# Five features of the mix stored as rounded and low parts, and two output tiles that take turns

## The chip, the cores and the metric

The kernel runs on one core of a Trainium2 chip. The metric is the time of one execution on the device in microseconds (us). Of the kernel before, three runs and one profiled execution are at hand. Its engines are TensorE (PE, with its weight loads as PEld), VectorE (DVE), ScalarE (ACT), GpSimd (POOL) and SyncE (SP); each works through its own instructions in order, and they meet at semaphores. Transfers between DRAM and the on-chip memory are DMAs, issued here from SP and POOL.

## The reference

Two encoder layers over 1040 frames of width 1024. In each layer a normed input goes through one projection whose columns serve two groups of heads: four gated-linear-attention heads (features 0 to 3 of the mix, 128 wide each) and eight softmax heads with a forget bias (FoX), which give features 4 to 7. The mix is what goes through the output projection `w_out`:

```python
xn = rms_norm(h, attn_norm[i])
gq, gk, gv, gr, glr, fq, fk, fv, ff = jnp.split(xn @ w_in[i], cuts, axis=-1)
o_gla = rms_norm(gla_chunk_causal(...), gla_norm[i]...) * jax.nn.silu(gr)
o_fox = rms_norm(forgetting_attention(...), fox_norm[i]...)
h = h + jnp.concatenate([o_gla, o_fox], axis=-1) @ w_out[i]
h = h + conv_ffn(rms_norm(h, ffn_norm[i]), w_up[i], conv_w[i], conv_b[i], w_down[i])
```

All of it is in float32.

## The kernel before

A float32 product is made of three matmuls of a rounded type (`mm3`, L241 to L243): each operand is split into a part `hi`, rounded by a cast on ACT, and a part `lo`, the rest, subtracted on DVE; PE then adds hi x hi, hi x lo and lo x hi. `split` (L366, L367, and with a scale L369, L370) does it for activations, `weights` (L208, L210) for weights. Features lie on the partitions (128 of them), frames along the rows.

The attention of a layer runs in `fox` as a fixed series of steps: four pairs of FoX heads, eighteen steps a pair, in five groups of query tiles (the last group has one tile). A step issues scores (`S`, L686, L687), DVE adds the bias row `cb` and keeps the running minimum (`P` and `m`, L694), ACT takes the exponential, PE transposes (`tr`, L723), ACT and DVE split the transposed block (`PT`), and PE multiplies with the values (`av`, L741). At the end of a group `fox_fold` transposes and norms (`fo`, `ff`), and two steps later `fox_store` transposes once more and writes the feature of the pair. The masks of `cb` run on POOL. PSUM tiles `S`, `tr` and `fo` share a ring of five buffers, the tile `mm` has two.

Between these steps stands filler work, so that PE does not run dry: `plan(p)` gives a list of units when pair p begins. A unit (`unit`) is one output tile of 128 columns over one chunk of frames and is taken matmul by matmul between the attention's own instructions. With pairs 0 to 2 the filler makes the projections of the next pair and the gate of head p (`gr_products`, with the gate's own chain `gx`, `ge`, `gy`, `gog` on DVE and ACT, L646 to L657); with pair 3, the gate of head 3. When that is done `plan(4)` gives the first four output tiles of `w_out` (`NSPLIT`), each over chunks of 256, 384 and 400 frames, and over seven of the eight features in the order KORD = (4, 5, 0, 1, 2, 3, 6). Feature 7, that of pair 3, is added later, in the next stage.

The mix gets there through DRAM: `fox_store` (L787, L788) and the gate (L657, L659) write each feature as float32 to `mixd[k]`; with `plan(3)` five of them are loaded into `land` on POOL (L970), feature 6 comes in chunks in `plan(4)` (L975), and feature 3 never leaves the chip. In `plan(4)` all seven are split, chunk by chunk, 21 splits (`mh` on ACT L366, `ml` on DVE L367) in each layer. The first output tile carries them: two splits are issued ahead of a unit (FEED = 2), then one with each feature. The residual stream is loaded into the same `land` tiles behind the split (L991, POOL) and added when the output is read from PSUM (L996). The next tile's weights are asked for when the first unit of a tile starts.

The instructions of each engine are recorded in the order in which this code issues them, but for the scores, which are moved up by some places.

## Time and profile before

| | us |
|---|---|
| median of three runs | 2553.93 |
| the runs | 2550.85, 2553.93, 2555.95 |
| profiled execution | 2549.59 |
| its span | 2547.7 |
| mean granted clock of PE | 0.994 |
| PE, DVE, ACT, POOL busy | 2483.9, 1748.1, 1273.1, 405.1 |

Times in the trace run from the start of the span. The attention of layer 0 ends near 500, that of layer 1 near 1790. Pair 3 of layer 0 begins near 412, and its `plan(4)` near 455. A row of the timeline reads: start, duration, engine, line, operation, what it writes and reads, and in brackets how long the engine stood idle before it and what ended that.

### The profile page before, as it was taken

The page shows a single profiled execution, that of the slowest core. Times are in us where ns is not written, and L with a number is a line of the kernel's source. Part 1 is how long each engine was busy: PE and PEld are TensorE (multiplying, and loading weights), DVE is VectorE, ACT ScalarE, POOL GpSimd, SP SyncE. Part 2 cuts the span into 40 slices and gives each one's busy share as a digit, 9 for nine tenths or more (in the row PEclk, how much of TensorE's full clock was granted, in tenths as well). Part 3 has the DMA queues.
Part 4 walks back from the last instruction along what each step waited for, and adds up shares of the span by engine and source line. Part 5 has one row for each costly group of instructions (what it writes and reads, how often), then busy time and mean ns, then how long its engine had stood idle before and what let it go on. Part 6 is the DMA issues. An engine that isn't in the chain of part 4 may idle for free.

```text
span 2547.7 us, 48524 instructions
## 1 busy us (share of the span) xinstructions
PE 2483.9 (97%) x19278; PEld 2420.5 (95%) x19278; DVE 1748.1 (69%) x3389; ACT 1273.1 (50%) x2582; POOL 405.1 (16%) x580
## 2 busy tenths in 40 slices
PE   8999999999999999999999999999999999999998
PEld 7989999998999999999999899999999999999997
DVE  7655676769877777853565666777697777777535
ACT  7346666646544445641343466665464444455412
POOL 4033333210000000100210333331100000001002
PEclk9999999999999999999999999999999999999999
DMA  3232134342322224764312222142523222258622
GB/s 122 71 86 73 39 95 129 114 152 78 107 86 78 81 80 127 201 161 116 106 50 72 74 79 68 66 148 95 169 74 110 75 76 87 76 158 187 187 70 76
DMA packets 118515, 260.91 MB, mean 102 GB/s; under 512 B 14880, under 2 KB 32544, under 8 KB 118288
## 3 DMA queue, kind: packets, MB, share of 16 engines
q1 hardware_dynamic: 95136, 184.36, 23.2%
q0 software_dynamic: 22432, 72.71, 10.4%
q8 instruction: 151, 2.47, 0.4%
q10 hardware_dynamic: 720, 0.74, 0.1%
q14 instruction: 76, 0.62, 0.1%
HBM read 177.16 MB, written 67.81 MB: 96 GB/s over the span
## 4 chain that ended last, share of the span: by engine, by line
PE 65%; issue 17%; DVE 11%; DMA 3%; ACT 3%; POOL 1%; SPq 0%; DVEq 0%; POOLq 0%; ACTq 0%
PE mm L241 8%; PE mm L243 7%; PE mm L242 7%; PE up L242 5%; PE up L241 5%; PE up L243 5%; PE down L241 5%; PE down L242 5%; PE down L243 5%; PE av L741 3%; PE tr L723 2%; DVE P L694 2%; DVE x L1085 1%; PE wo L241 1%; PE S L686 1%
## 5 line engine op out<-in xcount | busy, mean ns | idle before, releaser
L241 PE MATMUL up<-x,hi 128*128 128x260 f32 (+1 forms) x2464 | 699.2, 284 | 8.0 <-ACT hi L1060 4.9
L243 PE MATMUL up<-x,hi 128*128 128x260 f32 (+1 forms) x2464 | 698.0, 283 | 2.1 <-DVE x L1085 2.1
L242 PE MATMUL up<-x,lo 128*128 128x260 f32 (+1 forms) x2464 | 698.5, 283 | 1.3 <-DVE lo L1061 1.3
L241 PEld LDWEIGHTS up<-x,hi 128*128 128x128 f32 x2464 | 466.6, 189 | 9.7 <-ACT hi L1060 5.3
L243 PEld LDWEIGHTS up<-x,hi 128*128 128x128 f32 x2464 | 467.0, 190 | 3.0 <-DVE x L1085 2.9
L242 PEld LDWEIGHTS up<-x,lo 128*128 128x128 f32 x2464 | 466.5, 189 | 2.0 <-DVE lo L1061 1.8
L1061 DVE TENSOR_TENSOR lo<-raw,hi 128x512 fp32r<-128x512 f32 x364 | 247.6, 685 | 173.4 <-ACT hi L1060 173.4
L241 PE MATMUL mm<-xh,hi 128*128 128x348 f32 (+4 forms) x1056 | 363.4, 344 | 0.0
L243 PE MATMUL mm<-xl,hi 128*128 128x348 f32 (+4 forms) x1056 | 340.0, 322 | 0.0
L242 PE MATMUL mm<-xh,lo 128*128 128x348 f32 (+4 forms) x1056 | 339.5, 321 | 0.0
L1060 ACT CAST hi<-raw 128x512 fp32r<-128x512 f32 x364 | 224.3, 620 | 145.5 <-PE up L243 84.9
L241 PEld LDWEIGHTS mm<-xh,hi 128*128 128x128 f32 x1056 | 200.0, 189 | 6.3 <-issue 5.3
L242 PEld LDWEIGHTS mm<-xh,lo 128*128 128x128 f32 x1056 | 200.0, 189 | 0.6 <-issue 0.3
L243 PEld LDWEIGHTS mm<-xl,hi 128*128 128x128 f32 x1056 | 198.8, 188 | 0.9 <-issue 0.7
L208 ACT CAST hi<-raw 128x512 fp32r<-128x512 f32 (+2 forms) x184 | 106.6, 582 | 185.0 <-PE down L243 113.0
L242 PE MATMUL down<-ah,lo 128*128 128x260 f32 (+1 forms) x704 | 198.0, 281 | 0.6 <-DVE lo L210 0.5
L243 PE MATMUL down<-al,hi 128*128 128x260 f32 (+1 forms) x704 | 198.1, 281 | 0.0
L241 PE MATMUL down<-ah,hi 128*128 128x260 f32 (+1 forms) x704 | 198.0, 281 | 0.0
L367 DVE TENSOR_TENSOR PT<-tr,PT 116x464 fp32r<-116x464 f32 (+3 forms) x240 | 122.3, 515 | 71.3 <-ACT PT L366 69.2
L702 ACT ACTIVATE P<-P,m 116x924 f32<-116x924 f32 (+4 forms) x144 | 110.5, 767 | 75.0 <-DVE m L694 69.4
L723 PE MATMUL tr<-ident,P 116*116 116x116 f32 x704 | 144.0, 268 | 2.3 <-DVE m L694 1.8
L1268 POOL DMA_DIRECT2D actd<-cv x44 | 23.6, 536 | 766.5 <-DVE cv L1267 745.5
(283 smaller groups left out, 5768.3 us busy)
## 6 DMA issues: line engine op xcount, KB each, us to landing
raw<-in_wm_dram SPq DMA_DIRECT2D x330, 256.0 KB, 2.9
raw<-in_wd_dram SPq DMA_DIRECT2D x64, 256.0 KB, 3.7
actd<-cv POOLq DMA_DIRECT2D x22, 520.0 KB, 3.0
actd<-cv POOLq DMA_DIRECT2D x22, 512.0 KB, 3.1
cb<-cd SPq DMA_DIRECT2D x16, 520.0 KB, 4.2
st<-actd SPq DMA_DIRECT2D x14, 520.0 KB, 5.1
st<-actd SPq DMA_DIRECT2D x14, 512.0 KB, 5.9
kA<-kA SPq DMA_DIRECT2D x24, 260.0 KB, 4.4
```

The source lines that it names most:

```text
L208: nc.scalar.copy(hi[:, :n, :], raw[:, :n, :])
L241: nc.tensor.matmul(ps, wh, xh[:, c0:c0 + n], start=first, stop=False, skip_group_check=more)
L242: nc.tensor.matmul(ps, wl, xh[:, c0:c0 + n], start=False, stop=False, skip_group_check=more)
L243: nc.tensor.matmul(ps, wh, xl[:, c0:c0 + n], start=False, stop=last, skip_group_check=more)
L367: nc.vector.tensor_tensor(out=lo, in0=src, in1=hi.bitcast(F32), op=ALU.subtract)
L686: nc.tensor.matmul(S[:rows, :n], q["qA"][e][:, qs], q["kA"][e][:, c0:k1], start=True, stop=False)
L694: nc.vector.tensor_tensor_reduce(out=x, in0=S[:rows, :n], in1=cb[:rows, c0:k1], scale=1.0, scalar=(BIG if ci == 0 else m[:rows, ci - 1:ci] ...
L702: nc.scalar.activation(x, x, AF.Exp, scale=-1.0, bias=low, accum_out=(den if nch < 3 else d2[:rows, 0:1]))
L723: nc.tensor.transpose(tr[:w, j, :rows], P[:rows, o:o + w], id_)
L741: nc.tensor.matmul(av[:, a:width], w.rearrange("p a b -> p (a b)"), x, start=(t == 0 and i == 0), stop=(t == last and i == 1))
L1060: nc.scalar.copy(hi[:, :nk, :], src[:, :nk, :])
L1061: nc.vector.tensor_tensor(out=lo[:, :nk, :], in0=src[:, :nk, :], in1=hi[:, :nk, :].bitcast(F32), op=ALU.subtract)
```

## The change

Five features, PARTS = (4, 5, 0, 2, 6), are split where they are produced. In `fox_store` of pairs 0 to 2 ACT writes the rounded part to `fst` as before and DVE the low part into `on`, which is the tile `ff` of the fold (one buffer); in the gates of heads 0 and 2 ACT casts into `gog` and DVE subtracts into `gy` (one buffer). Two DMAs write the parts to `mixh` and `mixl`. With `plan(3)` six full loads bring the parts of 4, 5 and 0 straight into `mh` and `ml`, with one load for feature 1; in `plan(4)` twelve loads from SP bring features 2 and 6 chunk by chunk. Features 1 and 3 are still split in `plan(4)`: 6 splits instead of 21.

The first two output tiles take turns chunk by chunk. FEED = 8 issues the splits of a chunk in one go, and the second tile's units carry those of the chunk after. The next tile's weights are asked for in the last chunk of the second tile (`wait`, `left`).

```diff
@@ -53,3 +53,4 @@
 NSPLIT = 4
-FEED = 2
+PARTS = (4, 5, 0, 2, 6)
+FEED = 8
 N_DMA_SUM = 5
@@ -176,3 +177,4 @@
         self.hd = [dp.tile([128, T], F32, name=f"hd{k}") for k in range(KD)]
-        self.mixd = [dp.tile([128, T], F32, name=f"mixd{k}") for k in range(KD)]
+        self.mixd = dp.tile([128, T], F32, name="mixd1")
+        self.mixs = {k: [dp.tile([128, T], F32, name=f"mix{x}{k}") for x in "hl"] for k in PARTS}
         self.ogd = [dp.tile([128, T], F32, name=f"ogd{k}") for k in range(4)]
@@ -256,4 +258,4 @@
             f()
-        if not box.get("ahead"):
-            box["ahead"] = True
+        box["left"] = box.get("left", box["wait"] + 1) - 1
+        if box["left"] == 0:
             nxt = box["work"].after(box)
@@ -273,9 +275,17 @@
 
-    def add_tile(self, work, pp, src, xs, chunks, evac, ks=range(KD), w=None, feed=None, vec=False):
-        box = {"src": src, "work": work, "vec": vec}
-        if w is not None:
-            box["w"] = w
-        work.boxes.append(box)
+    def add_tile(self, work, pp, src, xs, chunks, evac, ks=range(KD), w=None, vec=False):
+        self.add_tiles(work, pp, [(src, evac, w, {})], xs, chunks, ks, vec)
+
+    def add_tiles(self, work, pp, tiles, xs, chunks, ks, vec):
+
+        boxes = []
+        for src, evac, w, feed in tiles:
+            box = {"src": src, "work": work, "vec": vec, "wait": len(chunks) - 1 if boxes else 0}
+            if w is not None:
+                box["w"] = w
+            boxes.append(box)
+        work.boxes += boxes
         for j, (c0, n) in enumerate(chunks):
-            work.add(self.unit(pp, box, src, ks, xs, c0, n, evac, (feed or {}).get(j, ())), len(ks) * 3 * mm_us(n))
+            for box, (src, evac, w, feed) in zip(boxes, tiles):
+                work.add(self.unit(pp, box, src, ks, xs, c0, n, evac, feed.get(j, ())), len(ks) * 3 * mm_us(n))
 
@@ -657,4 +667,9 @@
             nc.vector.scalar_tensor_tensor(out=to, in0=y, scalar=-1.0, in1=og, op0=ALU.mult, op1=ALU.mult)
-            if dst is None:
-                nc.gpsimd.dma_start(self.mixd[h][:, c0:c0 + n], e)
+            if h in PARTS:
+                parts = og, y
+                self.split(*(x.bitcast(F32R) for x in parts), e)
+                for d, x in zip(self.mixs[h], parts):
+                    nc.gpsimd.dma_start(d[:, c0:c0 + n], x)
+            elif dst is None:
+                nc.gpsimd.dma_start(self.mixd[:, c0:c0 + n], e)
         self.add_tile(work, pp, self.wm[lyr, M_GR + h], nm["x"], CH_FOX if dst is None else CH_FOX[::-1], ev)
@@ -785,5 +800,7 @@
             return
-        st = ap.tile([128, 2 * FT], F32, tag="fst", name="fst", bufs=1)
-        nc.scalar.mul(st[:, :n], trf[:, :n], self.v(lyr, V_XN, p))
-        nc.gpsimd.dma_start(self.mixd[4 + p][:, c0:c0 + n], st[:, :n])
+        parts = [x[:, :n] for x in (ap.tile([128, 2 * FT], F32, tag="fst", name="fst", bufs=1),
+                                    on.rearrange("p a b c -> p (a b c)"))]
+        self.split(*(x.bitcast(F32R) for x in parts), trf[:, :n], self.v(lyr, V_XN, p))
+        for d, x in zip(self.mixs[4 + p], parts):
+            nc.gpsimd.dma_start(d[:, c0:c0 + n], x)
 
@@ -957,2 +974,5 @@
                 box = {}
+
+                def part_slots(k):
+                    return s.get(F32R, f"mh{k}"), s.get(F32R, f"ml{k}")
                 KORD = (4, 5, 0, 1, 2, 3, 6)
@@ -967,10 +987,11 @@
                     elif p == 3:
-                        land = box["land"] = [s.get(F32, f"h{k}") for k in range(KD - 1)]
-                        for k in (4, 5, 0, 1, 2):
-                            nc.gpsimd.dma_start(land[k][:, :T], self.mixd[k][:])
+                        mix = box["mix"] = {k: part_slots(k) for k in PARTS[:3]}
+                        land = box["land"] = {k: s.get(F32, f"h{k}") for k in (3, 1)}
+                        for k in PARTS[:3]:
+                            for x, d in zip(mix[k], self.mixs[k]):
+                                nc.gpsimd.dma_start(x[:, :T].bitcast(F32), d[:])
+                        nc.gpsimd.dma_start(land[1][:, :T], self.mixd[:])
                         self.gr_products(lyr, 3, w, ap, pp, nm, land[3])
                     elif p == 4:
-                        land = box["land"]
-                        for c0, n in reversed(CH):
-                            nc.gpsimd.dma_start(land[6][:, c0:c0 + n], self.mixd[6][:, c0:c0 + n])
+                        mix, hT = box["mix"], box["land"]
                         for x in nm["x"]:
@@ -978,4 +999,18 @@
                         s.put(nm["r"])
-                        mix = box["mix"] = [(s.get(F32R, f"mh{k}"), s.get(F32R, f"ml{k}")) for k in range(KD)]
-                        hT = box["hT"] = land + [s.get(F32, "h7")]
+                        for k in (2, 6):
+                            mix[k] = part_slots(k)
+                        for c0, n in CH[::-1]:
+                            for k in (2, 6):
+                                for x, d in zip(mix[k], self.mixs[k]):
+                                    nc.sync.dma_start(x[:, c0:c0 + n].bitcast(F32), d[:, c0:c0 + n])
+                        mix[1] = part_slots(1)
+                        hT[0] = s.get(F32, "h0")
+                        mix[3] = part_slots(3)
+                        hT[2] = s.get(F32, "h2")
+                        mix[7] = part_slots(7)
+                        for k in range(4, KD):
+                            hT[k] = s.get(F32, f"h{k}")
+                        mix = box["mix"] = [mix[k] for k in range(KD)]
+                        hT = box["hT"] = [hT[k] for k in range(KD)]
+                        land = hT
                         ready = self.weights(self.wm[lyr, M_WO], vec=True)
@@ -991,9 +1026,12 @@
                                     nc.gpsimd.dma_start(hT[m][:, c0:c0 + n], hsrc[m][:, c0:c0 + n])
-                            return [lambda k=k: one(k) for k in KORD] + [residual]
-                        for m in range(NSPLIT):
-                            def ev(ps, c0, n, m=m):
+                            return [lambda k=k: one(k) for k in KORD if k not in PARTS] + [residual]
+                        def out_tile(m):
+                            def ev(ps, c0, n):
                                 h = hT[m][:, c0:c0 + n]
                                 nc.vector.tensor_tensor(out=h, in0=ps, in1=h, op=ALU.add)
-                            first = {} if m else {"w": ready, "feed": {j: split(2 - j) for j in range(3)}}
-                            self.add_tile(w, pp, self.wm[lyr, M_WO + m], mix, chunks[::-1], ev, ks=KORD, vec=True, **first)
+                            feed = {0: split(2)} if m == 0 else {j: split(1 - j) for j in range(2)} if m == 1 else {}
+                            return self.wm[lyr, M_WO + m], ev, None if m else ready, feed
+                        self.add_tiles(w, pp, [out_tile(0), out_tile(1)], mix, chunks[::-1], KORD, True)
+                        for m in range(2, NSPLIT):
+                            self.add_tiles(w, pp, [out_tile(m)], mix, chunks[::-1], KORD, True)
                     return w
```

How the order moves is shown at three places, all of layer 0.

The first is the start of the output projection on PE. `mm_6178` is the first tile over 256 frames; the rows begin with the last matmul of its last feature, 6, and run on into the next unit. Before:

```order
L243 MATMUL mm_6178<-ml6_6114,hi_6126 128x256
L723 MATMUL tr_6228<-ident_61,P_6030 116x116
L686 MATMUL S_6236<-kA0_4630,qA0_4628 116x460
L687 MATMUL S_6236<-kL0_4632,qA0_4628 116x460
L723 MATMUL tr_6228<-ident_61,P_6030 116x116 x3
L241 MATMUL mm_6247<-mh4_6109,hi_6126 128x384
```

The changed kernel (`mm_6244` is the first tile, `mm_6303` the second, both over 256 frames):

```order
L245 MATMUL mm_6244<-ml6_6155,hi_6188 128x256
L738 MATMUL tr_6280<-ident_61,P_6084 116x116
L701 MATMUL S_6288<-kA0_4660,qA0_4658 116x460
L702 MATMUL S_6288<-kL0_4662,qA0_4658 116x460
L738 MATMUL tr_6280<-ident_61,P_6084 116x116 x3
L243 MATMUL mm_6303<-mh4_5826,hi_6240 128x256
```

Around the scores nothing moves; behind them stands the second tile's chunk of 256 frames with the same `mh` and `ml` in place of the first tile's chunk of 384.

On DVE at the same place, up to the read of the scores that fill the buffer which the scores above take (`P_6154` before). `ml` rows are splits; `fa`, `fy`, `ff` belong to the fold. Before:

```order
L367 TENSOR_TENSOR ml2_6106<-h2_5779,mh2_6105 128x256
L312 TENSOR_TENSOR fa_6059<-fa_6059,fv_6056 116x4
L367 TENSOR_TENSOR ml3_6108<-h3_5780,mh3_6107 128x256
L313 SCALAR_TENSOR_TENSOR fy_6058<-fa_6059,fy_6058 116x4
L654 SCALAR_TENSOR_TENSOR ge_6086<-ge_6086,gy_6089 128x344
L769 TENSOR_TENSOR ff_6052<-ff_6052,fy_6058 116x128 x2
L655 SCALAR_TENSOR_TENSOR gy_6089<-ge_6086,gy_6089 128x344
L694 ISA P_6154,m_6150<-S_6151,cb_5485 116x460
```

The changed kernel (the read is `P_6216`):

```order
L377 TENSOR_TENSOR ml1_6169<-h1_5833,mh1_6168 128x384
L323 SCALAR_TENSOR_TENSOR fy_6112<-fa_6113,fy_6112 116x4
L377 TENSOR_TENSOR ml3_6172<-h3_5832,mh3_6171 128x384
L784 TENSOR_TENSOR ff_6106<-ff_6106,fy_6112 116x128 x2
L664 SCALAR_TENSOR_TENSOR ge_6140<-ge_6140,gy_6143 128x344
L709 ISA P_6216,m_6212<-S_6213,cb_5523 116x460
```

In front of the read stand four splits now, of features 1 and 3 for two chunks; before, it was seven. Behind the read and four rows more of the gate and the same scores the changed kernel has

```order
L377 TENSOR_TENSOR PT0_6202<-tr_6204,PT0_6202 116x4x116
L377 TENSOR_TENSOR ml1_6169<-h1_5833,mh1_6168 128x400
L377 TENSOR_TENSOR ml3_6172<-h3_5832,mh3_6171 128x400
L777 SCALAR_TENSOR_TENSOR fd_6437<-den_5861 116x4
L377 TENSOR_TENSOR PT1_6203<-tr_6264,PT1_6203 116x3x116
L1031 TENSOR_TENSOR h0_6170<-mm_6244,h0_6170 128x256
L709 ISA P_6291,m_6287<-S_6288,cb_5523 116x460
L709 ISA m_6287 116x1
L377 TENSOR_TENSOR PT0_6202<-tr_6280,PT0_6202 116x4x116
```

with the 400-frame splits of features 1 and 3 ahead of the `PT0` that the next `av` waits for; before, five splits stood there, and nine more behind it.

The second place is the end of pair 0 on DVE (`ff_3431` and `ff_3448` are the folds of its last group, `ge` and `gy` the gate's chain), with what each row waits for. Before:

```order
L657 SCALAR_TENSOR_TENSOR ge_3370<-gy_3373,gog_3368 128x348 [waits DVE_49]
L758 TENSOR_TENSOR ff_3431<-fo_3428,ff_3431 112x128 [waits Activation_49]
L646 TENSOR_TENSOR gx_3467<-mm_3383,r_149 128x348 [waits PE_49]
L367 TENSOR_TENSOR PT1_3323<-tr_3448,PT1_3323 116x4x116 [waits Activation_49]
L764 TENSOR_REDUCE fv_3435<-fo_3428 112x2 [waits Activation_49]
L653 TENSOR_TENSOR gog_3464<-gx_3467,gog_3464 128x348 [waits DMAHW7_49,DVE_49]
L765 TENSOR_TENSOR fv_3435<-fv_3435,fd_3436 112x2 [waits DVE_49]
L762 SCALAR_TENSOR_TENSOR fd_3746<-den_3193 116x4 [waits DVE_49]
L311 SCALAR_TENSOR_TENSOR fa_3438<-fy_3437 112x2 [waits Activation_49]
L649 TENSOR_SCALAR ge_3466<-gx_3467 128x348 [waits DMASW7_49]
```

The changed kernel:

```order
L667 SCALAR_TENSOR_TENSOR ge_3382<-gy_3385,gog_3380 128x348 [waits DVE_49]
L380 SCALAR_TENSOR_TENSOR ff_3312<-tr_3437,vec_59,fst_3440 128x232 [waits Activation_49]
L377 TENSOR_TENSOR PT1_3335<-tr_3465,PT1_3335 116x4x116 [waits Activation_49]
L377 TENSOR_TENSOR gy_3385<-ge_3382,gog_3380 128x348 [waits Activation_49]
L656 TENSOR_TENSOR gx_3484<-mm_3398,r_152 128x348 [waits PE_49]
L659 TENSOR_SCALAR ge_3483<-gx_3484 128x348 [waits DVE_49]
L663 TENSOR_TENSOR gog_3481<-gx_3484,gog_3481 128x348 [waits DMAHW7_49,DMASW0_49]
L773 TENSOR_TENSOR ff_3448<-fo_3445,ff_3448 112x128 [waits DMASW3_49,Activation_49]
L709 ISA P_3533,m_3529<-S_3530,cb_3196 116x460 [waits PE_49]
```

Two rows come in, the low parts of the fox store (`ff_3312`) and of the gate (`gy_3385`); the add of the fold moves down by six rows, and it now waits for a DMA too (DMASW3, the store of `ff_3312`). The `ge` of the next chunk no longer waits for a store.

The third place is the start of pair 3 on POOL, from the first load of a feature. Before:

```order
L970 DMA h4_5781<-mixd4_94 128x1040 [waits DMASW4_49,PE_49]
L970 DMA h0_5777<-mixd0_90 128x1040 [waits DMASW5_49]
L210 TENSOR_TENSOR lo_5825<-raw_5822,hi_5824 128x512 [waits DMAHW1_49,Activation_49]
L970 DMA h5_5782<-mixd5_95 128x1040 [waits DMASW6_49,DMAHW2_49,DMASW1_49,PE_49]
L859 TENSOR_TENSOR cb_5485<-cb_5485,mask_66 116x116 [waits DMAHW1_49,DVE_49,Pool_49]
L970 DMA h1_5778<-mixd1_91 128x1040 [waits DMASW7_49,DMASW0_49]
```

The changed kernel:

```order
L992 DMA mh5_5828<-mixh5_93 128x1040 [waits DMASW5_49,DMASW3_49,PE_49]
L992 DMA mh4_5826<-mixh4_91 128x1040 [waits DMASW4_49,PE_49]
L992 DMA mh0_5830<-mixh0_95 128x1040
L876 TENSOR_TENSOR cb_5523<-cb_5523,mask_66 116x116 [waits DMAHW1_49,DVE_49,Pool_49]
L992 DMA ml4_5827<-mixl4_92 128x1040 [waits DMASW6_49,PE_49]
L992 DMA ml5_5829<-mixl5_94 128x1040 [waits DMASW7_49]
```

Three loads stand ahead of the first mask of `cb` in both; in the changed kernel the low part of a weight tile no longer stands between them, and two more full loads follow behind the mask.

## The prediction

> **What bounds the kernel now.** The page comes first, then the windows of 10 us, then the chain of waits and the timeline of the places where a window shows TensorE idle.

> ```profile
> PE 2483.9 (97%) x19278; PEld 2420.5 (95%) x19278; DVE 1748.1 (69%) x3389; ACT 1273.1 (50%) x2582; POOL 405.1 (16%) x580
> ```

> TensorE (PE) is busy for 97% of the span, and the change takes no matmul away: 17561 rows of PE stand in the order before and after. All that can be won is idle time of PE, 63.8 us in a span of 2547.7, and time lost to a lowered clock. So I looked for the windows in which PE is idle near the code that the change touches (columns: busy us and count of PE, PEld, DVE, ACT, POOL, then the granted clock, the DMA share and GB/s).

> ```profile
> 460.00:470.00 10.00, 6.38 (x50) 5.64 (x48) 9.96 (x32) 10.00 (x28) 2.23 (x5) 1.00 0.53 166
> 470.00:480.00 10.00, 10.00 (x60) 9.70 (x61) 9.93 (x26) 4.18 (x13) 4.66 (x9) 0.83 0.50 155
> 1720.00:1730.00 10.00, 6.37 (x48) 5.79 (x48) 9.97 (x32) 10.00 (x29) 1.71 (x3) 0.85 0.48 150
> ```

> In each layer there is one window (460 to 470, 1720 to 1730) in which PE stands for 3.6 us while DVE and ACT are full: this is the start of the output projection, where the mix features are split. The waits of that stage and the rows of PE around them:

> ```profile
> PE mm L243 <- DVE ml L367: 3.6, 2, 3.0
> ...
> 462.45 0.36 PE L241 MATMUL mm<-mh,hi 128*128 128x256 f32 x1
> 463.95 0.78 PE L741 MATMUL av<-PT,V 116*128 116x232 f32 x6
> 465.94 0.39 PE L243 MATMUL mm<-ml,hi 128*128 128x256 f32 x1 [0.65 <-DVE ml L367]
> 469.94 0.38 PE L243 MATMUL mm<-ml,hi 128*128 128x256 f32 x1 [2.97 <-DVE ml L367]
> 471.73 0.52 PE L243 MATMUL mm<-ml,hi 128*128 128x384 f32 x1
> 472.05 0.52 PE L241 MATMUL mm<-mh,hi 128*128 128x384 f32 x1
> 474.55 0.34 PE L241 MATMUL mm<-mh,hi 128*128 128x384 f32 x1
> 474.73 0.34 PE L242 MATMUL mm<-mh,lo 128*128 128x384 f32 x1
> 1725.05 0.38 PE L243 MATMUL mm<-ml,hi 128*128 128x256 f32 x1 [0.67 <-DVE ml L367]
> 1729.04 0.58 PE L243 MATMUL mm<-ml,hi 128*128 128x256 f32 x1 [2.96 <-DVE ml L367]
> ```

> PE waits for the low part of a split twice, 0.65 and 2.97 us; layer 1 repeats it to 0.02 us. Behind it the clock is down: the 384-column matmuls start 0.32 us apart (471.73, 472.05) until about 474.1, and 0.18 us apart (474.55, 474.73) later. The granted clock of 470 to 480 is 0.83, so 0.17 of 10 us, **1.7 us** more, is lost in a layer. The place costs 3.62 + 1.7 = 5.3 us per layer, 10.6 us in both.

> **The change part by part, the splits first.**

> ```profile
> L367 DVE TENSOR_TENSOR ml<-h,mh x42: 408/545/568, 457.5 to 1737.6; 128x256 fp32r<-128x256 f32 x14, 128x384 fp32r<-128x384 f32 x14, 128x400 fp32r<-128x400 f32 x14
> L366 ACT CAST mh<-h x42: 388/508/544, 428.6 to 1729.8; 128x256 fp32r<-128x256 f32 x14, 128x384 fp32r<-128x384 f32 x14, 128x400 fp32r<-128x400 f32 x14
> L370 DVE SCALAR_TENSOR_TENSOR ml<-tr,vec,mh x10: 332/457/459, 474.5 to 1780.0; 128x232 fp32r<-128x232 f32 x8, 128x112 fp32r<-128x112 f32 x2
> ```

> Of 42 splits at 0.545 us on DVE and 0.508 us on ACT, 30 leave this stage (15 a layer, 8.2 us of DVE, 7.6 us of ACT); 12 stay. They come back as 30 operations of the L370 kind (0.457 us) in the fox pairs and 12 subtractions of about 0.5 us in the gates of heads 0 and 2, where DVE is less full. The count of DVE's work hardly changes; its place does.

> What is late next? In the changed order PE runs the same rows up to the end of the first unit (all seven features need only two splits now), and then meets a scores matmul that waits for DVE's read P of the scores before it. The rows of DVE in that stage:

> ```profile
> 461.72 0.42 DVE L758 TENSOR_TENSOR ff<-fo,ff 116x256 f32<-116x256 f32 x1
> 464.19 1.29 DVE L210 TENSOR_TENSOR lo<-raw,hi 128x512 fp32r<-128x512 f32 x2
> 467.68 0.63 DVE L694 CUSTOM_DVE_ANT_0 P<-S,cb 116x460 f32<-116x460 f32 x1
> 469.48 2.28 DVE L367 TENSOR_TENSOR ml<-h,mh 128x256 fp32r<-128x256 f32 x5
> ```

> Before, P starts at 467.68 with about 3.0 us of splits queued ahead of it since 457; after, four splits of 1.9 us stand there. So P starts about 1.1 us earlier, at 466.6, and is read out near 467.2. PE did four features from 462.45 to 463.95, 0.375 us each, and stood at the fifth at 464.81, after the av group and transposes; three features more and one transpose end at about 466.1. First new wait: **1.1 us**. Second: the next av group on PE waits for a PT split on DVE that stands behind the two 400-column splits, two more PT splits, the residual add and the next P. From 467.2 these sum to about 4.8 us (five at 0.43 to 0.55, two at 0.50, two at 0.3 to 0.35), to 472.0; PE gets there at 470.9. Second new wait: **1.1 us**. Together 2.2 us instead of 3.62: 1.4 us per layer won, with ends of 0 (DVE as late as before) and 3.6 (both waits gone).

> The clock: single stalls near 1.1 us, as these two would be, left it alone.

> ```profile
> 362.12 0.47 PE L686 MATMUL S<-kA,qA 128*116 128x460 f32 x1 [1.03 <-DVE m L694]
> 363.79 0.32 PE L242 MATMUL mm<-xh,lo 128*128 128x344 f32 x1
> 427.88 0.32 PE L741 MATMUL av<-PT,V 112*128 112x112 f32 x1 [1.11 <-DVE PT L367]
> ```

> After 1.03 us of idling the 344-column matmul still takes 0.32 us, as elsewhere at full clock. With 3.7 us of work between the two new waits I count the clock as kept: another 1.7 us a layer, ends 0 and 1.7. The splits' term is therefore 2 x (1.4 + 1.7) = **-6.2 us**.

> [...]

> The loads: features 2 and 6 arrive as parts by 12 loads from SP into slots that PE's last reads of xh0 to xl1 free at about 456.0, and are wanted at 464.8.

> ```profile
> 455.70 0.32 PE L243 MATMUL mm<-xl,hi 128*128 128x344 f32 x1
> 464.81 0.36 PE L241 MATMUL mm<-mh,hi 128*128 128x256 f32 x1
> h<-mixd POOLq DMA_DIRECT2D x1, 128.0 KB, 2.4
> ```

> Four loads of 128 KB, issued by 458 and 2.4 us long, are there by 460.5: hidden by 4 us, **0**. If that cover went, each us beyond 464.8 would stand on PE.

> **Pair ends.** The fold of the fifth group writes the one ff buffer, which now holds the low part of the fourth group's store until its DMA lands; ACT's copy waits for that, DVE's add waits for ACT, and on DVE P stands behind, and PE's next scores behind P. Pairs 0, 1 and 2 of two layers: six places.

> ```profile
> 269.95 0.28 DVE L758 TENSOR_TENSOR ff<-fo,ff 112x128 f32<-112x128 f32 x1
> 270.33 0.55 POOL L659 DMA_DIRECT2D mixd<-ge  x1 [0.61 <-DVE ff L758]
> 275.34 0.34 DVE L649 TENSOR_SCALAR ge<-gx 128x348 f32<-128x348 f32 x1 [2.01 <-DMA mixd<-ge]
> 276.19 0.63 DVE L694 CUSTOM_DVE_ANT_0 P<-S,cb 116x460 f32<-116x460 f32 x1
> 355.48 0.28 DVE L758 TENSOR_TENSOR ff<-fo,ff 112x128 f32<-112x128 f32 x1
> 359.85 0.63 DVE L694 CUSTOM_DVE_ANT_0 P<-S,cb 116x460 f32<-116x460 f32 x1
> DMA to landing us min/median/max: 1.8/3.3/5.3
> ```

> The last row is that of the fox stores (fst). At pair 1 the new operation takes the place of the add at 355.48, so the low part is ready near 355.9, lands 3.3 us later at 359.3, copy and add take 0.6: P at about 360.1, against 359.85, **+0.25 us**. At pair 0 of layer 0 DVE already waited for a store that took 5.0 us (270.33 to 275.34), and the new wait falls on the same time: about 0. I take 4 x 0.25 = **+1.0 us** for the six, with ends of -1.5 (pair 0's wait gone) and 6 x 2.2 = +13 (each store as slow as the slowest, 5.3 us).

> [...]

> **Start of pair 3.** POOL issues three loads of 520 KB ahead of the first mask of cb, as before, but the third without a weight subtraction in front of it, and seven loads in all instead of five.

> ```profile
> cb<-cd SPq DMA_DIRECT2D x16, 520.0 KB, 4.2
> 412.19 1.08 POOL L970 DMA_DIRECT2D h<-mixd  x2 [3.41 <-PE tr L723]
> 413.98 0.33 SPq L830 DMA_DIRECT2D cb<-cd  x1
> 416.27 0.57 POOL L970 DMA_DIRECT2D h<-mixd  x1
> 420.69 0.64 DVE L694 CUSTOM_DVE_ANT_0 P<-S,cb 116x460 f32<-116x460 f32 x1 [0.93 <-DMA cb<-cd]
> ```

> cb took 6.7 us from its issue to P beside these loads, against a median of 4.2 us, and DVE waited 0.93 us for it; PE's stall of 1.11 us at 427.88 lies behind. Three loads cost it 2.5 us, 0.8 us each; the third comes at about 413.3 now, ahead of cb and not 2.3 us behind it, and can cost at most those 0.8 us again, or nothing, if cb has its share of the engines whatever stands in POOL's queue. I take 0.3 us in each layer: **+0.6 us**. Last, the third tile's weights are made only when the second tile is in its last chunk, one unit (about 5 us) before use: two casts and two subtractions of 0.65 us each (L210 above) nearly always fit: **+0.6 us**, ends 0 and 4.

> The sum is -6.2 + 1.0 + 0.6 + 0.6 = **-4.0 us**. The profiled execution took 2549.59 us (span 2547.7 and 1.9 around it), 4.3 us below the median 2553.93 of three runs; I put the difference on the median: **2549.9 us**. About 0.2%, 5.1 us, is what a measurement of this kernel can tell from no change.

> **The rivals.**

> **Both waits vanish.** DVE turns out to be earlier than I add up, since the chain of casts on ACT gets shorter too (ACT is full from 460 to 470). For it: 1.1 us each is small. Then -10.6 + 2.2 = -8.4, 2545.5 us. Chance 0.20.

> **The clock drops all the same**, because the two waits lie 3.7 us apart. For it: between 465.94 and 469.94 two waits were 1 us apart and the clock fell. Against it: the two rows above. -2.8 + 2.2 = -0.6, 2553.3 us. Chance 0.12.

> **The change doesn't do what it says:** the wait for splits comes back whole, as a wait for P or for late part loads, with the clock loss. Then 0 + 2.2: 2556.1 us. Chance 0.10.

> **Slower: the stores hold ff.** At the pair ends the DMA writes of the low parts take as long as the one of 5.0 us at 270.33, two stores instead of one being queued. Each place costs 0.25 us plus what the landing takes over 3.3 us, so 2 us each, about 12 us in all, and -6.2 + 12 + 1.2 = +7.0: 2560.9 us. It is slower by more than 5.1 us from 10.1 us on the six places, 1.7 us each, a landing of 4.75 us. For it: max 5.3 and the stall at 275.34. Against it: the median 3.3. Chance 0.13.

> **How the numbers follow.** My forecast has 0.45; its own range is 2547 to 2553, of which somewhat under two fifths lies below 2548.8 (faster by 0.2%). Faster: 0.17 of it and the 0.20 of the first rival, 0.37. Slower: 0.12 of the last rival and 0.05 of the third, 0.17. The rest, 0.46, is within 0.2%. The range runs from 2544 (first rival with somewhat less given back) to 2559 (third rival), and leaves out most of the last.

> **What would show it.** In the profile after: no wait of mm for ml in the first unit of w_out, one or two waits of about 1.1 us of S for DVE m and of av for PT near 466 and 471, and a granted clock of 1.00 in 470 to 480; ACT's ff copy at 359 waiting for a store of a low part, by how much; P at the start of pair 3 waiting 1.2 us for cb. It is wrong if these waits are over 2 us at the pair ends, or if the windows at 460 and 1720 are as empty as before.

## The result and the profile after

| us | before | after |
|---|---|---|
| median | 2552.39 (2546.76 to 2555.95, 4 runs) | 2564.74 (2563.97 to 2567.83, 4 runs) |
| profiled execution, its span | 2549.59, 2547.7 | 2564.54, 2562.8 |
| mean granted clock of PE | 0.994 | 0.996 |

The change makes the kernel slower: ratio 1.0053, with the interval 1.0035 to 1.0071 (the two medians alone give 1.0048). The predicted 2549.9 us lies 14.8 us too low, and the time lies outside the range of 2544 to 2559.

The page of the changed kernel, span and busy times:

```profile
span 2562.8 us, 48708 instructions
PE 2483.8 (97%) x19278; PEld 2418.3 (94%) x19278; DVE 1762.1 (69%) x3401; ACT 1266.6 (49%) x2564; POOL 425.4 (17%) x620
```

PE is busy for 2483.8 us, where it was 2483.9, so the 15.1 us of span stand as idle time of PE: 79.0 us instead of 63.8. Where they arise is read best from one instruction that both kernels issue in the same order and number: DVE's read of scores (`P<-S,cb` and `P<-S,cb,m`, together 224 times). Its start in the rows of the timeline of DVE, at the ends of the stages (the third kernel is an experiment below):

| the read that stands in before at | where this is | after | later by | feature 0's loads on SP | later by |
|---|---|---|---|---|---|
| 188.67 | start of pair 0, layer 0 | 189.58 | 0.91 | 190.14 | 1.47 |
| 364.37 | behind the end of pair 1 | 364.68 | 0.31 | 364.64 | 0.27 |
| 458.13 | behind the end of pair 2 | 466.37 | 8.24 | 460.36 | 2.23 |
| 500.86 | end of pair 3 | 506.41 | 5.55 | 500.43 | -0.43 |
| 1452.05 | start of pair 0, layer 1 | 1456.68 | 4.63 | 1454.72 | 2.67 |
| 1624.22 | behind the end of pair 1 | 1630.95 | 6.73 | 1628.92 | 4.70 |
| 1712.07 | behind the end of pair 2 | 1728.80 | 16.73 | 1719.08 | 7.01 |
| 1760.57 | end of pair 3 | 1773.38 | 12.81 | 1763.61 | 3.04 |

The pairs overlap: in the changed kernel the first read of pair 3 stands near 422, the last fold of pair 2, which is what its end means here, near 449. (Layer 1's last reads stand near 1760, not near the 1790 given above.) Almost all of the loss comes in one stage in each layer, which holds the start of pair 3 and then the end of pair 2: 7.9 us in layer 0 (8.24 - 0.31) and 10.0 in layer 1. The output projection behind it gives back 2.7 and 3.9 us.

**The output projection** went much as predicted. The waits of that stage, its rows on PE and its first windows, in the changed kernel:

```profile
PE av L756 <- DVE PT L377: 1.7, 2, 1.0
PE S L701 <- DVE m L709: 1.4, 1, 1.4
...
469.67 1.05 PE L756 MATMUL av<-PT,V 112*128 112x232 f32 x7 [0.70 <-DVE PT L377]
476.66 0.46 PE L701 MATMUL S<-kA,qA 128*116 128x460 f32 x1 [1.41 <-DVE m L709]
481.24 1.05 PE L756 MATMUL av<-PT,V 112*128 112x232 f32 x7 [0.95 <-DVE PT L377]
...
460.00:470.00 10.00, 9.30 (x68) 8.91 (x67) 7.80 (x21) 6.02 (x15) 1.72 (x4) 1.00 0.50 140
470.00:480.00 10.00, 8.59 (x73) 8.16 (x72) 10.00 (x32) 7.69 (x20) 6.16 (x12) 1.00 1.00 345
```

The wait for splits is gone; the two waits that were forecast are there (1.41 and 0.95 us), with a third one of 0.70 that was not; and the granted clock is 1.00 where it was 0.83.

**The start of pair 3** is where the time goes. The timeline of the changed kernel, rows of DVE, POOL and PE, then two windows:

```profile
421.75 0.64 DVE L709 CUSTOM_DVE_ANT_0 P<-S,cb 116x460 f32<-116x460 f32 x1 [1.82 <-DMA cb<-cd]
421.78 0.43 POOL L876 TENSOR_TENSOR cb<-cb,mask 116x116 f32<-116x116 f32 x1 [7.65 <-DMA cb<-cd]
425.38 2.94 DVE L721 TENSOR_TENSOR den<-d 116x1 f32<-116x1 f32 x1 [1.18 <-ACT Ps L720]
425.40 1.30 POOL L212 TENSOR_TENSOR lo<-raw,hi 128x512 fp32r<-128x512 f32 x1
426.65 0.43 POOL L876 TENSOR_TENSOR cb<-cb,mask 116x116 f32<-116x116 f32 x1
427.03 1.26 POOL L212 TENSOR_TENSOR lo<-raw,hi 128x512 fp32r<-128x512 f32 x1
428.25 0.33 DVE L659 TENSOR_SCALAR ge<-gx 128x344 f32<-128x344 f32 x1
431.75 0.46 PE L756 MATMUL av<-PT,V 112*128 112x112 f32 x1 [4.79 <-DVE PT L377]
435.33 0.49 PE L245 MATMUL mm<-xl,hi 128*128 128x348 f32 x1
1688.30 0.64 DVE L709 CUSTOM_DVE_ANT_0 P<-S,cb 116x460 f32<-116x460 f32 x1 [2.13 <-DMA cb<-cd]
1691.92 2.96 DVE L721 TENSOR_TENSOR den<-d 116x1 f32<-116x1 f32 x1 [1.18 <-ACT Ps L720]
1698.31 0.46 PE L756 MATMUL av<-PT,V 112*128 112x112 f32 x1 [4.90 <-DVE PT L377]
430.00:440.00 10.00, 8.25 (x36) 7.60 (x37) 8.08 (x29) 6.10 (x19) 2.52 (x5) 0.66 0.39 129
1700.00:1710.00 10.00, 10.00 (x56) 9.36 (x55) 8.14 (x29) 6.55 (x17) 2.31 (x4) 0.77 0.33 106
```

The same place before, rows of POOL and DVE:

```profile
415.03 1.28 POOL L210 TENSOR_TENSOR lo<-raw,hi 128x512 fp32r<-128x512 f32 x1 [1.75 <-ACT hi L208]
421.79 1.30 POOL L210 TENSOR_TENSOR lo<-raw,hi 128x512 fp32r<-128x512 f32 x1
422.62 0.51 DVE L646 TENSOR_TENSOR gx<-mm,r 128x344 f32<-128x344 f32 x1
424.31 0.16 DVE L706 TENSOR_TENSOR den<-d 116x1 f32<-116x1 f32 x1 [1.18 <-ACT Ps L705]
```

`den` adds two numbers on each of 116 partitions. Before it takes 0.16 us; now, in both layers, it lasts 2.94 and 2.96 us, and it ends when POOL's second `lo` ends (427.03 + 1.26 = 428.29). The two `lo`, the low parts of the weights of head 3's gate, stood at 415.03 and 421.79, and no operation of DVE was held beside them; they stand at 425.40 and 427.03 now, behind the loads. All of DVE is late by 2.8 us behind `den`, PE waits 4.79 us for a split of DVE instead of 1.11, and its clock drops to 0.66 in the window behind that (348 columns take 0.49 us). Ahead of it, `cb` lands later: DVE waits 1.82 us for it instead of 0.93, and 2.13 us in layer 1, where it did not wait for it before.

A correction to the description of the kernel above: that each engine keeps the order in which the code issues is not so on POOL. Neither subtraction was moved by the code; both went behind the loads when a third load was put in front of the first mask.

### The profile page after: what moved, and what is told of

Its sections match the earlier page's. It is cut to its first block, busy times and chain, and to the rows that moved or that the text cites. A ratio compares the mean times of both kernels' runs of the same rounds, so it can differ in the third digit from the quotient of the medians.

```text
span 2562.8 us, 48708 instructions
## 1 busy us (share of the span) xinstructions
PE 2483.8 (97%) x19278; PEld 2418.3 (94%) x19278; DVE 1762.1 (69%) x3401; ACT 1266.6 (49%) x2564; POOL 425.4 (17%) x620
## 4 chain that ended last, share of the span: by engine, by line
PE 54%; issue 28%; DVE 11%; DMA 3%; ACT 2%; POOL 1%; SPq 0%; DVEq 0%; POOLq 0%; ACTq 0%
PE mm L243 8%; PE mm L244 7%; PE mm L245 7%; PE down L243 5%; PE down L244 5%; PE down L245 5%; PE av L756 3%; PE tr L738 2%; DVE P L709 1%; DVE cv L1274 1%; PE wo L243 1%; PE wo L245 1%; PE wo L244 1%; DVE x L1123 1%; PE S L701 1%
## 5 line engine op out<-in xcount | busy, mean ns | idle before, releaser
L243 PE MATMUL up<-x,hi 128*128 128x260 f32 (+1 forms) x2464 | 698.5, 284 | 8.4 <-ACT hi L1098 5.4
L243 PEld LDWEIGHTS up<-x,hi 128*128 128x128 f32 x2464 | 465.4, 189 | 10.2 <-ACT hi L1098 5.8
L243 PE MATMUL mm<-xh,hi 128*128 128x348 f32 (+4 forms) x1056 | 364.0, 345 | 0.0
L243 PEld LDWEIGHTS mm<-xh,hi 128*128 128x128 f32 x1056 | 200.7, 190 | 6.2 <-issue 5.3
L210 ACT CAST hi<-raw 128x512 fp32r<-128x512 f32 (+2 forms) x184 | 106.4, 581 | 186.4 <-PE down L245 112.0
L243 PE MATMUL down<-ah,hi 128*128 128x260 f32 (+1 forms) x704 | 197.9, 281 | 0.0
```

The lines of the kernel that those rows point to most:

```text
L210: nc.scalar.copy(hi[:, :n, :], raw[:, :n, :])
L243: nc.tensor.matmul(ps, wh, xh[:, c0:c0 + n], start=first, stop=False, skip_group_check=more)
```

## The experiments

Two theories stood for the loss at the start of pair 3. **Collision**: DVE is held by POOL's subtractions. **Late cb**: the third load ahead of `cb` delays the bias row, and everything follows from that. Medians are given with the ratio to the kernel before, timed on the same chip in the same series. The changed kernel was not timed again in these series, so a median "below the changed kernel" compares two series; the kernel before has medians of 2552.39, 2552.93, 2551.41 and 2552.46 us in the four, so such a difference is sure to some 1.5 us.

### The subtractions taken off POOL (lo_dve)

The low parts of head 3's gate weights on DVE; the loads stay:

```diff
-        self.add_tile(work, pp, ..., CH_FOX if dst is None else CH_FOX[::-1], ev)
+        self.add_tile(work, pp, ..., CH_FOX if dst is None else CH_FOX[::-1], ev, vec=dst is not None)
```

> The changed kernel, with the low parts of the weights of the last gate (head 3) subtracted on DVE in place of POOL. Theory 1 (collision: POOL's two subtractions, now late in its queue, hold a tiny DVE addition, den, for 2.9 us): den is back at 0.16 us in both layers, the av wait at the start of pair 3 falls from 4.8 and 4.9 us to about 2 us (1.1 and 0.5 before, plus cb later by 0.9 and 2.0 us), the clock behind it stays at 1.00; 2 x (2.8 + 3.4) = 12 us less than the changed kernel, about 2553 us. Rival (cb lands late behind more loads, and that alone makes the wait): the av wait stays above 4 us, about 2563 us.

Median 2561.21 (6 runs), ratio 1.0033 (1.0022 to 1.0045). `den` among the groups of DVE (min/median/max in ns), and the first read of scores in pair 3:

```profile
L722 DVE TENSOR_TENSOR den<-d x16: 150/155/161, 190.1 to 1698.2; 116x1 f32<-116x1 f32 x16
420.86 0.64 DVE L710 CUSTOM_DVE_ANT_0 P<-S,cb 116x460 f32<-116x460 f32 x1 [2.18 <-DMA cb<-cd]
```

Without POOL's work no `den` is above 161 ns, and PE's waits at the place fall from 4.79 and 4.90 to 2.4 and 1.6 us: the collision is real. `cb` stays late, and so do these waits, and the granted clock of 430 to 440 is 0.84: both theories hold a part. From behind pair 1 to behind pair 2 the reads of this kernel move by 4.3 us in layer 0 (from 0.97 early to 3.35 late) and by 4.4 in layer 1; with neither cause (next experiment) they move by 2.0 and 2.3. So in this profiled execution the late `cb` costs at most 2.4 + 2.1 = 4.5 us (DVE has the two subtractions on top here), and the collision the rest. The time was expected lower, at about 2553. The profiled execution, 2556.62, is the fastest of the six, 8.1 us below the median of after; the median is only 3.5 below it. Of the other five the time and the mean clock are on record (0.993 or 0.994, here 0.994) and no trace; what they lost stays open, and with it how much of the loss the collision has.

### Feature 0's loads on another queue (k0_sp)

The two loads of feature 0 on SP, all else as changed:

```diff
-                                nc.gpsimd.dma_start(x[:, :T].bitcast(F32), d[:])
+                                (nc.gpsimd if k else nc.sync).dma_start(x[:, :T].bitcast(F32), d[:])
```

> The changed kernel, with the two full loads of feature 0's parts issued from SP in place of POOL: one of them stands ahead of cb on SP, and on POOL the weight subtractions come ahead of the masks again, as in the kernel before. Theory 1 (collision): den takes 0.16 us, the av wait at the start of pair 3 is about 2 us, no clock loss, about 2553 us. Rival (cb's landing): cb is as late as in the changed kernel or later, since the same bytes are ahead of it, and the av wait stays above 4 us, about 2565 us.

Median 2554.40 (10 runs), ratio 1.0005 (0.9996 to 1.0015). PE, DVE and ACT have the same order as in the changed kernel; only POOL and SP differ, and POOL's subtractions are back between the loads. The timeline:

```profile
415.18 1.28 POOL L212 TENSOR_TENSOR lo<-raw,hi 128x512 fp32r<-128x512 f32 x1 [1.60 <-ACT hi L210]
420.89 0.64 DVE L709 CUSTOM_DVE_ANT_0 P<-S,cb 116x460 f32<-116x460 f32 x1 [0.99 <-DMA cb<-cd]
421.93 1.30 POOL L212 TENSOR_TENSOR lo<-raw,hi 128x512 fp32r<-128x512 f32 x1
424.52 0.16 DVE L721 TENSOR_TENSOR den<-d 116x1 f32<-116x1 f32 x1 [1.17 <-ACT Ps L720]
```

One edit of a queue takes 10.3 us off the median and removes the long `den` (0.16 us), the late `cb` (0.99 us) and the loss of clock (granted 1.00 in 430 to 440 and in 1700 to 1710). The table above then parts the stage: what this kernel still loses between the ends of pairs 1 and 2, 2.0 and 2.3 us, belongs to the end of pair 2; the rest, 7.9 - 2.0 = 6.0 and 10.0 - 2.3 = 7.7 us, is the start of pair 3, **13.7 us** in both layers. By the profiled executions up to 4.5 of it is the late `cb`, and 9.2 or more the collision. By the medians `lo_dve` wins back 3.5 us of the 10.3 that `k0_sp` does. No run brings `cb` in time and leaves the collision, so how the sum parts is not shown.

### Which operations are held (den1)

`den` by a reduction of one operand instead of an addition of two:

```diff
-            nc.vector.tensor_tensor(out=den, in0=d2[:rows, 0:1], in1=d2[:rows, 1:2], op=ALU.add)
+            nc.vector.tensor_reduce(out=den, in_=d2[:rows, 0:2], op=ALU.add, axis=AX.X)
```

> The changed kernel, with den added by a reduction over its two columns (one SBUF input) in place of an addition of two SBUF inputs. If what POOL's subtraction holds up on DVE are operations with two SBUF inputs: den takes about 0.2 us, and the next operation with two SBUF inputs, the gate's gog, is held in its place, for 1.3 to 2.5 us in place of 0.5; the av wait stays near 4 us, 2561 to 2565 us. If den waits for something else (its operand, a semaphore): it still takes 2.9 us.

One run: 2568.79 us, above the 2561 to 2565 that were expected. The timeline:

```profile
427.16 0.15 DVE L721 TENSOR_REDUCE den<-d 116x1 f32<-116x2 f32 x1 [1.17 <-ACT Ps L720]
427.20 1.30 POOL L212 TENSOR_TENSOR lo<-raw,hi 128x512 fp32r<-128x512 f32 x1
427.25 3.06 DVE L659 TENSOR_SCALAR ge<-gx 128x344 f32<-128x344 f32 x1
428.83 1.27 POOL L212 TENSOR_TENSOR lo<-raw,hi 128x512 fp32r<-128x512 f32 x1
```

The reduction goes through in 0.15 us, and the next operation, `ge`, is held in its place: 3.06 us instead of 0.33. I had expected that of `gog`, one later, since `ge` has a single input. So the hold doesn't come from what `den` waits for, nor from operations with two inputs alone.

### The fold's own buffer (ff_own)

The last group's fold in the tile `avs`, so that it needn't wait for the store of a low part:

```diff
-        f = ap.tile([128, 2, 2, 64], F32, tag="ff", name="ff", bufs=1)
+        if nt == 1:
+            f = avs.rearrange("p a b -> p (a b)")[:, :128].rearrange("p (t e d) -> p t e d", t=1, e=2)
+        else:
+            f = ap.tile([128, 2, 2, 64], F32, tag="ff", name="ff", bufs=1)
```

> The changed kernel, with the fold of a pair's last group (one tile) written into the av1 tile of that group in place of the one ff buffer, so that it waits for no store. Theory 2 (the one ff buffer, held by the store of the low part, costs at the ends of pairs): ACT's ff copy waits for no DMA, the tr waits of 2.3 and 2.8 us near 455 and 1715 fall below 0.7 us, pairs 0 and 1 gain up to 0.5 us each; 4 to 6 us less than the changed kernel, about 2560 us; the 4.8 us waits at the start of pair 3 stay. Rival (DVE's added work there makes these waits): they stay within 0.5 us, 2564 us.

Median 2568.93 (4 runs), ratio 1.0065 (1.0050 to 1.0080): slower than the changed kernel, where about 2560 was expected. What this edit takes away is seen in the changed kernel at the end of pair 2, on ACT and PE:

```profile
449.39 0.27 ACT L772 COPY ff<-fo 112x128 f32<-112x128 f32 x1 [1.28 <-DMA mixl<-ff]
455.75 0.32 PE L795 MATMUL tr<-ident,ff 112*128 112x112 f32 x1 [2.31 <-DVE PT L377]
456.55 0.32 PE L244 MATMUL mm<-xh,lo 128*128 128x348 f32 x1
1717.31 0.59 ACT L661 ACTIVATE gy<-ge,ones 128x348 f32<-128x348 f32 x1 [1.92 <-DMA mixl<-gy]
1722.68 0.32 PE L795 MATMUL tr<-ident,ff 112*128 112x112 f32 x1 [2.81 <-DVE PT L377]
```

In layer 0 ACT's copy of the fold waits for the store of the fox low part (`mixl<-ff`). In layer 1 that copy doesn't wait; ACT's `gy` does, for the store of the gate's low part. PE's waits there fall from 2.31 and 2.81 us to 1.00 and 0.98 in this experiment. But at pair 0 another store is in the way, in this experiment's timeline:

```profile
273.28 1.30 POOL L212 TENSOR_TENSOR lo<-raw,hi 128x512 fp32r<-128x512 f32 x1
274.52 0.56 POOL L672 DMA_DIRECT2D mixl<-gy  x1
278.15 0.59 ACT L661 ACTIVATE gy<-ge,ones 128x348 f32<-128x348 f32 x1 [2.25 <-DMA mixl<-gy]
283.43 0.32 PE L798 MATMUL tr<-ident,avs 112*128 112x112 f32 x1 [3.68 <-DVE PT L377]
```

The gate's low part lies in `gy`, which has one buffer too; its store is issued behind a subtraction on POOL now, ACT waits for it, and PE stands 3.68 us.

### Both buffers freed (low_own)

`ff_own`, and the gate's low part in `gx`, which has two buffers:

```diff
-                parts = og, y
+                parts = og, x
```

> ff_own, and in the gates of heads 0 and 2 the low part written into gx (two buffers) in place of gy (one buffer), so that neither fold nor gate waits for a store. Theory 2 in its wider form (two single buffers are held by the stores of low parts, and with one freed the other holds the same chain on ACT): ACT waits for no store at the ends of pairs; the tr waits of 3.7 and 3.9 us that ff_own had at pair 0 fall below 1 us, those of 2.3 and 2.8 near 455 and 1715 stay gone; the waits of 4.8 at the start of pair 3 stay; about 2558 us, 6 less than the changed kernel. Rival (DVE's added work, or POOL's subtraction holding DVE, makes the waits at the pair ends): over 2 us of them stay at pair 0, 2564 us.

Median 2557.73 (10 runs), ratio 1.0020 (1.0010 to 1.0030), 7.0 us below the changed kernel. Neither ACT nor DVE waits for a store at a pair's end any more (PE's waits are 0.5 us at most in 250 to 300 and 0.2 in 440 to 460); at the start of pair 3 PE's waits of 5.0 and 4.9 us stay. So the loss at the start of pair 3 doesn't hang on the stores.

### Both repairs together (best)

`low_own` and `k0_sp`.

> low_own and k0_sp together. If the two causes are all that the change lost, what is left is the gain in the output projection, 0.8 us of waits and 1.7 us of clock a layer, and what the ends of pairs win: den at 0.16 us, the start of pair 3 as before (1.2 and 0.4 us), no ACT wait for a store; 2546 to 2549 us, 4 to 7 us below the kernel before. Rival (a third cost is hidden): 2553 us or more.

Median 2548.66 (12 runs), ratio 0.9987 (0.9979 to 0.9996): 16.1 us below the changed kernel, against 10.3 + 7.0 = 17.3 for the two alone. With these two repairs the parts are no longer slower than before. One of the losses is not wholly gone: `den` takes 0.16 and 0.28 us at the start of pair 3 in the two layers, but in layer 1 DVE waits 1.92 us for `cb` at the start of pair 3 and PE 2.27 us behind it, as in the changed kernel and not in `k0_sp`.

### Taking turns alone, and the parts alone (alt_only, parts_only)

`alt_only` is the kernel before with the output tiles taking turns, FEED = 8, the splits a chunk ahead and the late weights; the mix is stored as before. `parts_only` is the changed kernel with its four tiles one after another:

```diff
-                            feed = {0: split(2)} if m == 0 else {j: split(1 - j) for j in range(2)} if m == 1 else {}
+                            feed = {} if m else {j: split(2 - j) for j in range(3)}
...
-                        self.add_tiles(w, pp, [out_tile(0), out_tile(1)], mix, chunks[::-1], KORD, True)
-                        for m in range(2, NSPLIT):
+                        for m in range(NSPLIT):
```

> The kernel before with the second half of the change alone: the first two tiles take turns, FEED is 8, the splits come a chunk ahead, the next weights late; all seven features still go through DRAM as float32 and are split, 21 a layer. Theory 1 and 2 put the loss on the parts: start of pair 3 and ends of pairs as before (den 0.16 us), the output projection still waits about 3 us for DVE, 2549 to 2554 us. Rival (the new order of tiles and weights loses time): 2558 us or more.

> The changed kernel with the four output tiles one after the other, as before (FEED 8, the first tile's units carry the splits of their own chunk). The collision (den 2.9 us, av waits of 4.8) and the waits at the ends of pairs stay, the waits of the output projection are within 1.5 us a layer of the changed kernel's 3.1: 2563 to 2568 us. If the taking of turns carried the gain there: they are 5 us a layer with the clock lost, 2570 us.

`alt_only`: 2548.00 (10 runs), ratio 0.9984 (0.9974 to 0.9993), below the 2549 to 2554 expected. `parts_only`: 2565.79 (4 runs), ratio 1.0055 (1.0039 to 1.0070), with the collision and 3.4 us of waits in the output projection (1.4 for S, 2.0 for `av`), as in the changed kernel (1.4 and 1.7). So the parts carry the whole loss, and beside them taking turns adds nothing measurable. By itself it gains 0.16%. The rows of PE in `alt_only`, and its window:

```profile
467.31 0.69 PE L694 MATMUL S<-kA,qA 128*116 128x460 f32 x1 [1.92 <-DVE m L702]
468.99 0.42 PE L242 MATMUL mm<-mh,lo 128*128 128x256 f32 x1
471.28 0.28 PE L242 MATMUL mm<-mh,lo 128*128 128x256 f32 x1
460.00:470.00 10.00, 8.08 (x57) 7.51 (x57) 10.00 (x32) 10.00 (x29) 1.72 (x3) 0.87 0.48 151
```

The wait is 1.92 us instead of 2.97 + 0.65, and the clock is still lost behind it (256 columns take 0.42 us, then 0.28). And even with all repairs the parts (`best`, 2548.66) are no faster than this, in the same series.

### The gate's store from the other buffer (alt_x, before_x)

The wait at the end of pair 0 is in the kernel before, too: DVE's `ge` waits 2.01 us for the store of `ge` in the quoted rows of the prediction. So the gate's result goes to `gx` there, in `alt_only` (`alt_x`) and in the kernel before (`before_x`), where the edit is the whole change:

```diff
-            to = e if dst is None else dst[:, c0:c0 + n]
+            to = x if dst is None else dst[:, c0:c0 + n]
...
-                nc.gpsimd.dma_start(self.mixd[h][:, c0:c0 + n], e)
+                nc.gpsimd.dma_start(self.mixd[h][:, c0:c0 + n], x)
```

> alt_only, and in the gates of heads 0 to 2 the float32 result written into gx (two buffers) in place of ge (one buffer), so that the next ge waits for no store. If DVE's wait of 2.0 us for the store at the end of pair 0 of layer 0 (275.34 in the kernel before) is what makes PE's waits of 1.4 and 1.3 us there: these fall to about 0.5 us in all and the clock in 280 to 290 stays at 1.00, 2 to 3.5 us less than alt_only, 2545 us. Rival (the fold or POOL's subtraction sets P there): the waits stay, 2548 us.

> The kernel before with that edit alone. The same 2 to 3.5 us at the end of pair 0 of layer 0, the rest as before, the output projection's waits of 0.65 and 2.97 us included: 2548 to 2550 us where the kernel before has 2551.4. Rival: no change.

`alt_x`: 2545.26 (11 runs), ratio 0.9973 (0.9962 to 0.9984), the fastest of all, below both kernels. `before_x`: 2550.46 (11 runs), ratio 0.9990 (0.9981 to 0.9999), a little above the 2548 to 2550 expected. PE's waits between 250 and 300 in `alt_x`:

```profile
PE S L694 <- DVE m L702: 0.6, 1, 0.6
PE tr L731 <- DVE m L702: 0.4, 1, 0.4
```

Before they are 1.4 and 1.3 us there, with a stretch of lowered clock behind (granted 0.50 from 279.75 to 283.16, 1.7 us lost); in `alt_x` the granted clock of 280 to 290 is 1.00.

## Why the prediction was wrong

The terms of the sum beside what the table of reads gives, in us for both layers:

| term | predicted | measured | from |
|---|---|---|---|
| splits and late weights (500.86, 1760.57) | -6.2 + 0.6 | -6.6 | -2.7 - 3.9 |
| pair ends | +1.0 | +5.8 | -0.6 + 2.1 (pairs 0 and 1), 2.0 + 2.3 (pair 2) |
| start of pair 3 | +0.6 | +13.7 | 6.0 + 7.7 |
| stretches that the change leaves alone | 0 | +2.3 | 0.91, 4.63 - 5.55, 15.1 - 12.81 |

But for rounding the measured column sums to 15.1 us, the difference of the spans.

**Start of pair 3: the step that failed.** The prediction named the fact: "the third without a weight subtraction in front of it". It priced what this does to `cb` and did not ask where the subtraction went. Two of them went 10 and 5 us later, on top of an addition of DVE that PE's next `av` hangs on. The instruction to follow was the one that had moved away. With the late `cb` that makes 13.7 us (`k0_sp`); by the profiled executions at least 9.2 of them are the hold (`lo_dve`), by the medians perhaps less. The `cb` part was mis-sized too: 0.3 us a layer with an upper end of 0.8; in layer 0 DVE's wait for `cb` grew by 0.9 us (1.82 - 0.93), in layer 1 the read waited 2.13 us for it where it had waited 0.23 us for PE, and up to 2.4 and 2.1 us of the time go with it (`lo_dve`). The other terms stayed between the ends given for them, but for the clock of the output projection in layer 1 (below).

The hold could have been read in the kernel before, at the end of pair 0:

```profile
270.90 1.30 POOL L210 TENSOR_TENSOR lo<-raw,hi 128x512 fp32r<-128x512 f32 x1
271.32 1.27 DVE L653 TENSOR_TENSOR gog<-gx,gog 128x348 f32<-128x348 f32 x1
```

Mostly `gog` takes 0.51 us; beside this subtraction it takes 1.27, and at 356.86, beside that of pair 1, 1.26. So the trace of the kernel before already held rows of DVE that are too long beside POOL's subtractions.

**Pair ends: the mechanism was right for one of two buffers, the size was not.** ACT's copy waits for the store of the fox low part, as said, in layer 0 (0.64 us at pair 0, 1.28 at pair 2); at pair 2 of layer 1 it is the gate's `gy` that waits, 1.92 us. The fourfold 0.25 us became 2.0 and 2.3 us at pair 2 alone, where PE waits 2.31 and 2.81 us; waits of over 2 us there were the prediction's own sign of being wrong. The rival "stores hold ff" needed 10.1 us at these places to be decided, and they cost 5.8. The forecast that pair 0's own wait would fall on the same time was nearly right in layer 0 (the read of 291.03 is 0.38 us early where that of 188.67 was 0.91 late: 1.3 us gained, by the clock, of which the kernel before loses 1.7 us there and the changed one nothing) and wrong in layer 1 (6.22 late at 1542.13 after 4.63 at 1452.05: 1.6 lost); that `gy`, the second single buffer, was now held by a store as well was not seen; the row at 1717.31 and `ff_own` show it.

**Splits: right in the sum.** Two waits of 1.1 us were forecast, and 1.41 and 0.95 came, with 0.70 for an `av` ahead of them; the clock was kept, as assumed (granted 1.00). So 3.62 us of waits became 3.06, a gain of 0.6 and not 1.4 us a layer, and the clock gave most of the rest: 1.7 us in layer 0 and 3.4 in layer 1. The sum had counted 1.7 there too, but the kernel before lost clock in two windows of that stage (granted 0.85 in 1720 to 1730, 0.81 in 1730 to 1740). So the waits gave 1.6 us less than forecast in both layers and the clock 1.7 more, and the two misses cancel. The second wait came out near the forecast by luck: the nine operations that are said to take about 4.8 us sum, at the durations given, to 3.8 to 4.4, which would have made it 0.1 to 0.8 us. The 0.6 us for late weights didn't come: no wait of PE in that stage is for weights, in either layer. The rival "the clock drops all the same" did not come for this kernel, but did for `alt_only` (1.92 us). Loads of features 2 and 6: hidden, as said; no row of the stage waits for one.

What stays open: how the 13.7 us part between the hold and the late `cb`, why `cb` lands late in some profiles and layers and not in others, why `lo_dve` lies only 3.5 us below the changed kernel in its median, and the 2.3 us in stretches that the change does not touch. The clock doesn't explain these 2.3: between 500 and 1500 it was at 0.50 for 6.8 us in the kernel before (580.1 to 586.9) and nowhere in the changed one.

## What to carry to other kernels

When an instruction disappears from between two others in a queue, find where it stands now and what runs on the neighbouring engine at that time; here that move, on an engine that is busy for 16% of the span, and the late `cb` beside it cost 13.7 us, twice the 6.6 that the output projection gained. Before a result gets a second reader by DMA, count the buffers of each tile that is stored: here two tiles with one buffer each made the store's landing a wait of the next producer (1.28 us for `ff`, 1.92 us for `gy`), and freeing one of them only showed the other (2.25 us in `ff_own`). And try the part of a change that adds no traffic by itself first: taking turns, with one store moved to a tile with two buffers, is 0.27% faster than the kernel before and needs none of the parts.

## What the runs showed of the hardware

The clock does not follow the length of a single wait: it was lost behind 1.92 us (`alt_only`, 0.87) and 2.97 us (before, 0.83), and kept behind 2.31 and 2.81 us (changed kernel at 455.75 and 1722.68; granted 1.00 in 450 to 460 and in 1720 to 1740). Where the clock is lost in the kernel before, up to the end of the attention of layer 1, the windows read 0.50 for 3.4 us (279.75 to 283.16, 470.90 to 474.31), or for twice that (580.13 to 586.95, 1727.01 to 1733.83). The starts of these stretches lie whole multiples of 3.413 us apart: 56 from 279.75 to 470.90, 88 to 580.13, 424 to 1727.01; in the changed kernel 371 from 431.40 to 1697.75. Two stretches of 3.4 us of the kernel before, counted from its loss at 470.9, and two of the changed one, counted in such steps from the loss at 431.4:

```profile
467.50:470.90 3.40, 0.96 (x7) 0.86 (x8) 3.40 (x11) 3.40 (x10) 0.64 (x2) 1.00 0.28 87
470.90:474.30 3.40, 3.40 (x15) 3.30 (x14) 3.40 (x9) 2.29 (x7) 1.51 (x3) 0.50 0.38 109
451.80:455.20 3.40, 1.64 (x11) 1.35 (x9) 2.59 (x9) 1.80 (x9) 0.34 (x1) 1.00 0.00 1
455.20:458.60 3.40, 2.85 (x21) 2.81 (x22) 3.19 (x10) 2.17 (x7) 1.19 (x3) 1.00 0.42 128
```

In the stretch ahead of the loss PE is busy for 0.96 of 3.4 us, in `alt_only` (464.0 to 467.4) for 1.48; where the clock is kept, for 1.64, since the wait of 2.31 us is cut in two by the end of the stretch at 455.2. So how busy PE was in such a stretch fits these rows, and the length of a wait does not. It is no sharp limit: 1.81 of 3.4 us (before, 1723.6 to 1727.0) lost the clock too, and `k0_sp` lost it at 1357.2 behind a stretch in which PE was busy throughout.
